# SwiGLU by Strassen products: the weight sums moved from GpSimd to VectorE, with more places for the first weight parts, later splits, and the last tile done for both halves at once

## The chip, the cores and the metric

The kernel runs on one core of one Trainium2 chip. The metric is the device time of one execution in microseconds (us). TensorE (PE) multiplies matrices, VectorE (DVE), ScalarE (ACT) and GpSimd (POOL) work on tiles in SBUF, SyncE (SP) issues most DMAs; GpSimd issues some too. Each engine runs its own instructions in a fixed order and waits on semaphores for the others.

## The reference

One inference step of a two-layer decoder trunk: layer 0 mixes tokens with an mLSTM, layer 1 with latent attention, and each is followed by a dense SwiGLU FFN. The part that matters here is the FFN, on T = 1032 tokens (1024 of a prompt and 8 of decoding requests), D_MODEL = 1024, D_FF = 2816, all in float32:

```python
def rmsnorm(x, g):
    x32 = x.astype(jnp.float32)
    y = x32 * lax.rsqrt(jnp.mean(x32 * x32, axis=-1, keepdims=True) + EPS)
    return (y * g.astype(jnp.float32)).astype(x.dtype)

def swiglu(x, w_gate_up, w_down):
    g, u = jnp.split(x @ w_gate_up, 2, axis=-1)
    return (jax.nn.silu(g) * u) @ w_down
...
        hp = hp + swiglu(rmsnorm(hp, norm_ffn[layer]), ffn_w_gate_up[layer], ffn_w_down[layer])
        hs = hs + swiglu(rmsnorm(hs, norm_ffn[layer]), ffn_w_gate_up[layer], ffn_w_down[layer])
```

## The kernel before

**Precision.** A float32 value is kept as a high part and a low part. `split` makes them: ScalarE copies the value rounded to the high part (L117), VectorE subtracts it to get the low one (L118). Each product is then three matmuls (`mm3`): high × high (L134), high × low of the activations (L135), low of the weights × high (L136). So the third matmul of a group can start only when VectorE's subtract is done, while the first two need only ScalarE's copy.

**Halves and tiles.** The tokens are in two halves of 512 and 520, each of two columns (256 and 260 wide, `PW`). D_FF is cut into 22 tiles of 128 (`NF`), named f = 0 to 21. The layer's normalised activations are made by a generator (`forms`) as seven sums and differences per half, each split: f0 to f6 hold half 0 (f7 also serves), c0 to c5 hold half 1.

**Gate and up, one tile.** `gate_up(wg, f, parts)` computes gate and up of a tile by seven Strassen products (`PRODUCTS`) instead of eight. For each product four pieces of k run through `mm3`, for half 0 and then for half 1, into the PSUM banks `sc`. So a tile for both halves is 7 × 2 × 4 × 3 = 168 matmuls. The results are gathered by ScalarE's copies and VectorE's additions into the tiles `u` and `gt` (L1050 to L1064), and silu and the product are applied there.

**Weights.** `operands` (L986 on) is a generator that yields the seven weight parts of a tile in the order of the products. It issues two loads of 512 KB on SyncE's queue into tiles `wr` (a11, a12 of the gate in the first, a21, a22 of up in the second). Four sums of 128x512 are formed: s = a21 + a22 (L1007), s3 = a11 − a21 (L1008), s − a11 (L1012) and a12 − s (L1015), all on GpSimd, called S in the rows. s and s3 need the second load. Each part is split by `put` into a place of 128 × 1024; there are three places, two of tag `wh` and one of tag `w3`, taken in turn, so a part's split waits for the end of the product that used the place three parts earlier. In the rows, places print as `wh`, `w` (that is `w3`) and `wl`. `gate_up` keeps one part made ahead of the product that runs.

**Down.** `down` is a generator over 36 steps of 14 products of `mm3` each (again Strassen, on pairs of f tiles), with operands `dA` to `dD` (weights loaded as `dr`, sums dS L1093 to L1096) and b (factors made from u by `spread`, L1072 to L1078, and split). Its PSUM banks are `mm` and `ss`, emptied at L1132 to L1143 into `wl` (two tiles of the tag `wl`, called st0) and `st`, and added to the result in DRAM by accumulating DMAs that GpSimd issues (L1144). `gate_up` calls it between its own products: after every second piece of k (a checkpoint) it takes one or more entries.

**The order of the FFN** (`ffn`): tiles 0 and 1 for half 0 are done before it, while the norm of half 1 is made. Then tile 2 for both halves, tiles 0 and 1 for half 1, tile 3 for both halves with the first two steps' entries of `down` (skip the first checkpoint, then two a checkpoint), tiles 4 to 19 with one entry a checkpoint, the rest of `down`. The last four tiles (18 to 21) are not fed to `down`: `keep` splits their u whole into tiles `a`, and plain down products (`last_products`) follow, in `to_mla` for layer 0 and `finish` for layer 1. Layer 1's tile 21 is done for half 0 and then again for half 1, with the loads, sums and splits of its weights each time; layer 0's is done once for both halves.

The instructions' order on each engine is set by a scheduler from the order of the code, its own costs and the tiles' places.

Of the kernel before, what the change touches and what calls it, by code (L numbers as in the profile page):

```python
# [28 lines left out]
NF = DFF // P  # L29
# [62 lines left out]
class Kern:  # L92
# [896 lines left out]
    def operands(self, wg, f):  # L989
        nc = self.nc  # L990
# [7 lines left out]
        def put(x):  # L998
            self.no += 1
            pool, tag = (self.wp, "wh") if self.no % 3 else (self.gu, "w3")  # L1000
            w = self.t(pool, [P, KT * P], tag, F32R).rearrange("p (i k m) -> p i k m", i=2, m=P)
            self.split(w[:, 0], w[:, 1], x)
            return w

        G = nc.gpsimd.tensor_tensor
        s, s3 = (self.t(self.gu, [P, 4, P], "S", bufs=2) for i in range(2))
# [13 lines left out]

    def gate_up(self, wg, f, parts, down=iter(()), skip=0, steps=1):
        nc = self.nc
        V = nc.vector
        gu = self.gu
        banks = {}
        U, X = {}, {}
        ops = self.operands(wg, f)
        ahead = next(ops)
        for s, bank, first in PRODUCTS:
            w, ahead = ahead, next(ops, None)  # L1030
            for i in parts:
# [5 lines left out]
                for k in range(4):  # L1037
                    self.mm3(ps, w[:, 0, k], w[:, 1, k], xh[:, k], xl[:, k], bool(first) and k == 0, k == 3, skip_group_check=True)
                    if k % 2:
                        if skip:  # L1040
                            skip -= 1
                        else:
                            for _ in range(steps):
                                next(down, None)
                if s == 0:
# [111 lines left out]
    def ffn(self, layer):  # L1157
# [12 lines left out]
        g = self.down(wd)  # L1170
        next(g)
        self.gate_up(wg, 3, (0, 1), g, 1, 2)
        for f in range(4, NF - 2):
# [8 lines left out]
        def keep(f, i):  # L1182
            o = lambda x: x[:, 512 * i:512 * i + 2 * PW[i]].rearrange("p (c t) -> p c t", c=2)
            self.split(o(self.act[f][0]), o(self.act[f][1]), self.u[f, i])

        for f in fs[:2]:
            for i in range(2):
                keep(f, i)
        for f in fs[2:]:
            for parts in ((0,), (1,)) if layer and f == NF - 1 else ((0, 1),):  # L1190
                self.gate_up(wg, f, parts)
                for i in parts:
                    keep(f, i)
        self.fc.release()
# [822 lines left out]
```

## Time and profile before

| | us |
|---|---|
| median of 3 runs | 2763.43 |
| lowest, highest | 2760.77, 2763.75 |
| profiled execution | 2736.87 |
| its span (first to last instruction) | 2735.1 |
| mean granted TensorE clock | 0.972 |
| FFN of layer 0 from tile 2 on (start of its products) | from 548.6 |
| FFN of layer 1 likewise | from 2015 |
| layer 1's tile 21 | 2639.25 to 2669.76 |

The profile is of one execution, and 1.8 us of it lie outside the span. A timeline row gives the start, the duration, the engine, the line, the operation, its output and inputs, the count, and in brackets the idle time before it and what ended that. Matmuls overlap, so a matmul's cost is the distance between starts and not its duration. A row of windows gives per engine the busy time and the count of instructions.

### The profile page before, as it was taken

How to read it: one execution, taken by the hardware profiler on the slowest of the kernel's cores; microseconds unless marked ns; L12 is line 12 of the kernel's file. 1: busy time of each engine (PE TensorE's matmuls, PEld its weight loads, DVE VectorE, ACT ScalarE, POOL GpSimd, SP SyncE). 2: the span in 40 equal slices, each digit the busy share in tenths (PEclk: the TensorE clock that was granted, in tenths of full speed). 3: DMA queues.
4: the chain of work that ended last, by engine and by line, in shares of the span. 5: the costliest groups of instructions: out<-in, count | busy, mean ns of one | idle time of the engine just before them, and what ended most of it. 6: DMA issues, size and time to landing. Idle time of an engine off the chain costs nothing. (4 is left out here: it accounts for less than half of the span.)

```text
span 2735.1 us, 54524 instructions
## 1 busy us (share of the span) xinstructions
PE 2553.6 (93%) x21151; PEld 2398.4 (88%) x21151; DVE 1884.8 (69%) x4321; ACT 1320.8 (48%) x3287; POOL 824.9 (30%) x762
## 2 busy tenths in 40 slices
PE   8999998979999999999889889888989999999988
PEld 8998976979999999999877677677988999999988
DVE  4345668868777778666558777685676877777755
ACT  4212334446555555454345464555345555555542
POOL 1000102223333333322336454442223333333332
PEclk9999989999999999999989999899999999999999
DMA  5133454416565655643667776555424566655652
GB/s 186 39 77 89 127 147 115 154 51 128 117 129 113 132 110 112 125 154 98 229 222 270 260 261 209 202 206 168 137 71 104 113 124 127 121 117 117 128 132 102
DMA packets 344073, 384.43 MB, mean 141 GB/s; under 512 B 23449, under 2 KB 276766, under 8 KB 335494
## 3 DMA queue, kind: packets, MB, share of 16 engines
q0 software_dynamic: 59520, 183.34, 28.6%
q1 hardware_dynamic: 259894, 181.25, 22.1%
q10 hardware_dynamic: 24400, 16.36, 2.3%
q8 instruction: 166, 2.72, 0.4%
q14 instruction: 93, 0.76, 0.1%
HBM read 255.17 MB, written 125.70 MB: 139 GB/s over the span
## 5 line engine op out<-in xcount | busy, mean ns | idle before, releaser
L117 ACT ACTIVATE wh<-wr 128x512 fp32r<-128x512 f32 (+2 forms) x176 | 141.4, 804 | 224.4 <-PE mm L135 129.5
L1144 POOL DMA_DIRECT2D x_d<-wl x72 | 86.7, 1204 | 315.3 <-DVE wl L1143 250.0
L1795 DVE STREAM_TRANSPOSE tt<-nat 128x1024 f32<-128x1024 f32 x128 | 153.6, 1222 | 13.1 <-DMA nat<-in_cache_latent_dram,idx 6.9
L118 DVE TENSOR_TENSOR b<-u,b 128x256 fp32r<-128x256 f32 (+1 forms) x252 | 135.5, 542 | 16.7 <-ACT b L117 16.7
L1007 POOL TENSOR_TENSOR S<-wr 128x512 f32<-128x512 f32 x45 | 70.1, 1559 | 254.7 <-DMA wr<-in_ffn_w_gate_up_dram 230.5
L1012 POOL TENSOR_TENSOR S<-S,wr 128x512 f32<-128x512 f32 x45 | 63.0, 1401 | 245.0 <-DVE wh L118 166.2
L118 DVE TENSOR_TENSOR wl<-wr,wh 128x1024 fp32r<-128x1024 f32 (+2 forms) x83 | 99.2, 1195 | 42.7 <-ACT wh L117 30.9
L117 ACT ACTIVATE b<-u 128x256 fp32r<-128x256 f32 (+1 forms) x252 | 98.4, 415 | 43.0 <-DVE u L1060 15.4
L118 DVE TENSOR_TENSOR wh<-S,wh 128x512 fp32r<-128x512 f32 x121 | 86.2, 712 | 34.7 <-ACT wh L117 32.8
L134 PE MATMUL mm<-zh,wh 128*128 128x344 f32 x320 | 104.3, 326 | 4.2 <-DVE ot L462 4.2
L135 PE MATMUL mm<-zl,wh 128*128 128x344 f32 x320 | 103.6, 324 | 0.0
L136 PE MATMUL mm<-zh,wl 128*128 128x344 f32 x320 | 103.3, 323 | 0.0
L1144 POOL DMA_DIRECT2D x_d<-st x72 | 99.9, 1388 | 7.0 <-ACT b L117 6.1
L117 ACT ACTIVATE wh<-S 128x512 fp32r<-128x512 f32 x121 | 76.5, 633 | 48.1 <-PE sc L136 28.6
L1802 PE MATMUL ss<-tt,qbd 128*32 128x128 f32 x2560 | 88.2, 279 | 8.6 <-DVE tt L1795 7.0
L1802 PEld LDWEIGHTS ss<-tt,qbd 128*32 128x32 f32 x2560 | 70.9, 111 | 21.5 <-DVE tt L1795 15.9
L1093 DVE TENSOR_TENSOR dS<-dr 128x128 f32<-128x128 f32 x72 | 48.0, 667 | 59.4 <-DMA dr<-in_ffn_w_down_dram 56.6
L1698 PE MATMUL mm<-wh,vt 128*128 128x256 f32 (+1 forms) x320 | 76.9, 302 | 10.7 <-ACT wh L117 6.0
L134 PE MATMUL sc<-zh,wh 128*128 128x344 f32 x256 | 84.0, 329 | 0.2 <-DVE q L432 0.2
L850 POOL TENSOR_TENSOR ss<-ss,sq 128x512 f32<-128x512 f32 (+2 forms) x36 | 49.5, 1374 | 113.4 <-ACT sq L849 113.1
L135 PE MATMUL sc<-zl,wh 128*128 128x344 f32 x256 | 83.0, 324 | 0.0
L136 PE MATMUL sc<-zh,wl 128*128 128x344 f32 x256 | 82.9, 324 | 0.0
(1002 smaller groups left out, 10949.6 us busy)
## 6 DMA issues: line engine op xcount, KB each, us to landing
wr<-in_ffn_w_gate_up_dram SPq DMA_DIRECT2D x98, 512.0 KB
x_d<-st POOLq DMA_DIRECT2D x72, 520.0 KB, 8.4
x_d<-wl POOLq DMA_DIRECT2D x72, 512.0 KB, 6.2
dr<-in_ffn_w_down_dram SPq DMA_DIRECT2D x72, 256.0 KB
wr<-in_mlstm_w_in_dram SPq DMA_DIRECT2D x24, 512.0 KB
wr<-in_mlstm_w_out_dram SPq DMA_DIRECT2D x16, 512.0 KB
wr<-in_mla_w_o_dram SPq DMA_DIRECT2D x15, 512.0 KB
q<-qn_d SPq DMA_DIRECT2D x28, 256.0 KB
```

Source lines behind the costliest of these rows:

```text
L117: ins = nc.scalar.activation(hi, src, AF.Copy)
L118: self.low = e.tensor_tensor(lo, src, hi.bitcast(F32), op=ALU.subtract)
L134: mm(ps, wh, xh, start=start, stop=False, **kw)
L135: mm(ps, wh, xl, start=False, stop=False, **kw)
L136: self.last = mm(ps, wl, xh, start=False, stop=stop, **kw)
L850: (V if d == KT - 1 else nc.gpsimd).tensor_tensor(SS[:, cs], SS[:, cs], sq, op=ALU.add)
L1007: G(s, a21, a22, op=ALU.add)
L1012: G(s, s, a11, op=ALU.subtract)
L1144: nc.gpsimd.dma_start(self.x_d[:, 2 * dp:2 * dp + 2, 512 * i:512 * i + 2 * PW[i]], st[i], accum_op=ALU.add)
L1698: nc.tensor.matmul(o, x, y, start=i == 0, stop=i == len(ops) - 1)
L1795: V.transpose(out=tt, in_=src.rearrange("p s (c i) -> p c s i", i=32))
L1802: nc.tensor.matmul(psS[32 * j:32 * j + 32, u * P:u * P + P], self.qbd[:, b, cb], tt[:, c, 4 * j:4 * j + 4].rearrange("p s k -> p (s k)"), ...
```

## The change

1. The four sums of `operands` are made by VectorE (`G = nc.vector.tensor_tensor`). GpSimd keeps its DMAs.
2. For tiles 0, 1 and 2 (f < 3) the parts go to five places in turn instead of three: `wh`, `wl`, `w3`, `wh`, `wl`; the two `wl` tiles are those that `down` takes for its results later. For these tiles two parts are made ahead, for the others one. The other tiles have the same three places as before.
3. In tile 3, `down` starts after five checkpoints, at 54 entries to 23 checkpoints, instead of after one at two a checkpoint.
4. The splits of the four last tiles: tile 18 is split ahead of tile 20, tile 19 within tile 20, tiles 20 and 21 after tile 21; before, 18 and 19 ahead of tile 20, and 20 and 21 each behind its own products.
5. Layer 1's tile 21 is done for both halves at once. Its weights are loaded, summed and split once.

The lines of the functions shift by two or three: L1007, L1008, L1012, L1015 are L1009, L1010, L1014, L1017; L1050 is L1053, L1058 to L1064 are L1061 to L1067, L1139 is L1142.

```diff
@@ -997,12 +997,14 @@
         def put(x):
             self.no += 1
-            pool, tag = (self.wp, "wh") if self.no % 3 else (self.gu, "w3")
+            tags = ("wh", "wl", "w3", "wh", "wl") if f < 3 else ("wh", "w3", "wh")
+            tag = tags[self.no % len(tags)]
+            pool = self.gu if tag == "w3" else self.wp
             w = self.t(pool, [P, KT * P], tag, F32R).rearrange("p (i k m) -> p i k m", i=2, m=P)
             self.split(w[:, 0], w[:, 1], x)
             return w
 
-        G = nc.gpsimd.tensor_tensor
+        G = nc.vector.tensor_tensor
         s, s3 = (self.t(self.gu, [P, 4, P], "S", bufs=2) for i in range(2))
         G(s, a21, a22, op=ALU.add)
         G(s3, a11, a21, op=ALU.subtract)
@@ -1018,16 +1020,18 @@
-    def gate_up(self, wg, f, parts, down=iter(()), skip=0, steps=1):
+    def gate_up(self, wg, f, parts, down=iter(()), skip=0, steps=(1, 1)):
...
+        cp = done = 0
         ops = self.operands(wg, f)
-        ahead = next(ops)
+        ahead = [next(ops) for _ in range(2 if f < 3 else 1)]
         for s, bank, first in PRODUCTS:
-            w, ahead = ahead, next(ops, None)
+            ahead.append(next(ops, None))
+            w = ahead.pop(0)
...
                     if k % 2:
-                        if skip:
-                            skip -= 1
-                        else:
-                            for _ in range(steps):
-                                next(down, None)
+                        cp += 1
+                        while done * steps[1] < steps[0] * (cp - skip):
+                            next(down, None)
+                            done += 1
@@ -1169,7 +1172,7 @@
-        self.gate_up(wg, 3, (0, 1), g, 1, 2)
+        self.gate_up(wg, 3, (0, 1), g, 5, (54, 23))
@@ -1183,14 +1186,13 @@
-        for f in fs[:2]:
+        for i in range(2):
+            keep(fs[0], i)
+        self.gate_up(wg, fs[2], (0, 1), (keep(fs[1], i) for i in range(2)))
+        self.gate_up(wg, fs[3], (0, 1))
+        for f in fs[2:]:
             for i in range(2):
                 keep(f, i)
-        for f in fs[2:]:
-            for parts in ((0,), (1,)) if layer and f == NF - 1 else ((0, 1),):
-                self.gate_up(wg, f, parts)
-                for i in parts:
-                    keep(f, i)
```

How the order of the instructions moves, at three places. First VectorE at the start of layer 0's tile 2, before: c5l is the last low part of the norm that the place begins with, `wh` the low part of a11 and later of a12, b and u belong to the factors of `down`. A row is line, operation, output, inputs, size, and the engines waited for.

```order
L118 TENSOR_TENSOR c5l_5586<-x_4738,c5h_5585 128x1040 [waits Activation_49]
L118 TENSOR_TENSOR wh_5636<-wr_5628,wh_5636 128x512 [waits DMAHW2_49]
L118 TENSOR_TENSOR b_5603<-u_5286,b_5603 128x256 [waits Activation_49]
L118 TENSOR_TENSOR b_5607<-u_5438,b_5607 128x256 [waits Activation_49]
L1072 TENSOR_TENSOR u_5286<-u_5286 128x256 [waits DVE_49]
L118 TENSOR_TENSOR b_5625<-u_5438,b_5625 128x256 [waits Activation_49]
L1076 TENSOR_TENSOR u_5286<-u_5438,u_5286 128x256 [waits DVE_49]
L118 TENSOR_TENSOR b_5610<-u_5286,b_5610 128x256 [waits Activation_49]
L118 TENSOR_TENSOR wh_5639<-wr_5628,wh_5639 128x512
```

The same place in the changed kernel, where a11's low part is written to a place of the tag `wl`:

```order
L1009 TENSOR_TENSOR S_5632<-wr_5630 128x512 [waits DMAHW3_49]
L118 TENSOR_TENSOR b_5603<-u_5286,b_5603 128x256 [waits Activation_49]
L118 TENSOR_TENSOR b_5607<-u_5438,b_5607 128x256 [waits Activation_49]
L1075 TENSOR_TENSOR u_5286<-u_5286 128x256 [waits DVE_49]
L118 TENSOR_TENSOR b_5625<-u_5438,b_5625 128x256 [waits Activation_49]
L1079 TENSOR_TENSOR u_5286<-u_5438,u_5286 128x256 [waits DVE_49]
L118 TENSOR_TENSOR b_5610<-u_5286,b_5610 128x256 [waits Activation_49]
L1010 TENSOR_TENSOR S_5633<-wr_5628,wr_5630 128x512 [waits DMAHW2_49]
L1077 TENSOR_TENSOR u_5286<-u_5438,u_5286 128x256 [waits DVE_49]
L118 TENSOR_TENSOR b_5619<-u_5286,b_5619 128x256 [waits Activation_49]
L1081 TENSOR_TENSOR u_5438<-u_5438,u_5286 128x256 [waits DVE_49]
L118 TENSOR_TENSOR wl_5636<-wr_5628,wl_5636 128x512
```

a11's low part, directly behind c5l before, now stands behind the two sums and nine operations on b and u.

Second, VectorE in a steady tile of layer 0, before (this is the place at 829.6 us of the trace; `wh_9228` is the low part of the next tile's a11, `w_9231` that of a12, L1139 empties a bank of `down`):

```order
L1058 TENSOR_TENSOR u_8882<-u_8882,sc_8915 128x260 [waits Activation_49]
L118 TENSOR_TENSOR wh_9228<-wr_9220,wh_9228 128x512 [waits DMAHW6_49,Activation_49]
L118 TENSOR_TENSOR dA_9138<-dr_9056,dA_9138 128x256 [waits Activation_49]
L1060 TENSOR_TENSOR u_8846<-u_8846,sc_8817 128x256 [waits PE_49]
L118 TENSOR_TENSOR b_9141<-u_8846,b_9141 128x256 [waits Activation_49]
L118 TENSOR_TENSOR b_9153<-u_8440,b_9153 128x256 [waits Activation_49]
L1060 TENSOR_TENSOR u_8882<-u_8882,sc_8849 128x260 [waits PE_49]
L118 TENSOR_TENSOR w_9231<-wr_9220,w_9231 128x512 [waits Activation_49]
L118 TENSOR_TENSOR b_9168<-u_8482,b_9168 128x260 [waits Activation_49]
L118 TENSOR_TENSOR dB_9182<-dS_9058,dB_9182 128x256 [waits Activation_49]
L1139 TENSOR_TENSOR wl_6158<-wl_6158,ss_9048 128x256 [waits Activation_49]
```

And in the changed kernel, where `wr_9222` is the second load:

```order
L1009 TENSOR_TENSOR S_9224<-wr_9222 128x512 [waits DMAHW0_49]
L118 TENSOR_TENSOR dA_9138<-dr_9056,dA_9138 128x256 [waits Activation_49]
L1010 TENSOR_TENSOR S_9225<-wr_9220,wr_9222 128x512 [waits DMAHW6_49]
L1063 TENSOR_TENSOR u_8846<-u_8846,sc_8817 128x256 [waits PE_49]
L118 TENSOR_TENSOR wh_9228<-wr_9220,wh_9228 128x512
L118 TENSOR_TENSOR b_9141<-u_8846,b_9141 128x256 [waits Activation_49]
L118 TENSOR_TENSOR b_9153<-u_8440,b_9153 128x256 [waits Activation_49]
L1063 TENSOR_TENSOR u_8882<-u_8882,sc_8849 128x260 [waits PE_49]
L118 TENSOR_TENSOR wh_9231<-wr_9220,wh_9231 128x512 [waits Activation_49]
L118 TENSOR_TENSOR b_9168<-u_8482,b_9168 128x260 [waits Activation_49]
L118 TENSOR_TENSOR dB_9182<-dS_9058,dB_9182 128x256 [waits Activation_49]
L1142 TENSOR_TENSOR wl_6158<-wl_6158,ss_9048 128x256 [waits Activation_49]
```

S, which waits for the second load, stands where a11's low part was, and ahead of everything down to the emptied bank.

Third, ScalarE in layer 0's tile 20, before: S_13375 and S_13376 are sums of the tile's weights, the four `a` are the splits of tiles 18 and 19, and the copies to u free the banks of the tile's first product.

```order
L117 ACTIVATE w_13421<-S_13375 128x512 [waits PE_49,Pool_49]
L117 ACTIVATE wh_13481<-S_13376 128x512 [waits PE_49,Activation_49]
L117 ACTIVATE a_13355<-u_12600 128x512
L117 ACTIVATE a_13355<-u_12642 128x520
L117 ACTIVATE a_13357<-u_13006 128x512
L117 ACTIVATE a_13357<-u_13042 128x520 [waits DVE_49]
L1050 COPY u_13398<-sc_13385 128x256 [waits DVE_49]
```

And in the changed kernel:

```order
L117 ACTIVATE wh_13421<-S_13371 128x512 [waits DVE_49,PE_49,Activation_49]
L117 ACTIVATE w_13481<-S_13372 128x512 [waits PE_49,Activation_49]
L117 ACTIVATE a_13355<-u_12600 128x512
L117 ACTIVATE a_13355<-u_12642 128x520
L117 ACTIVATE a_13357<-u_13006 128x512
L117 ACTIVATE a_13357<-u_13042 128x520
L1053 COPY u_13398<-sc_13381 128x256 [waits DVE_49]
```

The four splits stand where they stood, ahead of the copy.

## The prediction

> **What bounds the kernel now.** I read the head of the page first: TensorE (PE) is busy almost all of the span, VectorE (DVE) two thirds, GpSimd (POOL) a third.
>
> ```profile
> span 2735.1 us, 54524 instructions
> PE 2553.6 (93%) x21151; PEld 2398.4 (88%) x21151; DVE 1884.8 (69%) x4321; ACT 1320.8 (48%) x3287; POOL 824.9 (30%) x762
> ```
>
> So an edit can only win the places where PE stands still or runs at half clock. To price a matmul at full speed I took a stretch of TensorE's timeline without waits, the last weight tile (21) of layer 0, 168 matmuls:
>
> ```profile
> 1174.03 0.28 PE L134 MATMUL sc<-f0h,wh 128*128 128x256 f32 x1
> 1194.05 0.32 PE L134 MATMUL sc<-a,wh 128*128 128x344 f32 x1
> ```
>
> 20.02 us / 168 = 0.119 us each. With that I priced two stretches by windows (columns: window, its length, then busy us and count of PE, weight loads, DVE, ACT, POOL): the start of layer 0's FFN, and sixteen of its later tiles.
>
> ```profile
> 548.60:617.00 68.40, 52.07 (x381) 49.76 (x379) 46.90 (x82) 29.92 (x66) 17.57 (x14) 0.90 0.18 51
> 640.00:1140.00 500.00, 491.20 (x4060) 484.77 (x4060) 384.12 (x903) 283.78 (x777) 170.16 (x132) 1.00 0.62 122
> ```
>
> The start needs 381 × 0.119 = 45.3 us and takes 68.4: 23 us are lost. The steady part needs 4060 × 0.119 = 483 of 500: 17 us lost, about 1 us a tile. So the start of each layer is the worst place, and a steady tile has next to nothing to give.
>
> **The start (two parts ahead, five places; sums on VectorE).** TensorE's timeline names the waits (the bracket is the idle time before a row and its releaser):
>
> ```profile
> 548.61 0.28 PE L134 MATMUL sc<-f0h,wh 128*128 128x256 f32 x1
> 548.97 0.28 PE L135 MATMUL sc<-c0l,wh 128*128 128x260 f32 x1
> 553.16 0.58 PE L134 MATMUL sc<-f4h,wh 128*128 128x256 f32 x1 [3.91 <-ACT wh L117]
> 557.07 0.58 PE L136 MATMUL sc<-f0h,wh 128*128 128x256 f32 x1 [2.69 <-DVE wh L118]
> 561.49 0.28 PE L134 MATMUL mm<-b,dA 128*128 128x256 f32 x1
> 565.64 0.38 PE L134 MATMUL sc<-f3h,wh 128*128 128x256 f32 x1 [0.77 <-ACT wh L117]
> 576.07 0.39 PE L136 MATMUL sc<-f5h,w 128*128 128x256 f32 x1 [1.73 <-DVE w L118]
> 585.76 0.39 PE L134 MATMUL sc<-c3h,wh 128*128 128x260 f32 x1 [1.04 <-ACT wh L117]
> 600.74 0.39 PE L134 MATMUL sc<-c3h,w 128*128 128x260 f32 x1 [3.38 <-ACT w L117]
> 617.02 0.39 PE L134 MATMUL mm<-b,dB 128*128 128x260 f32 x1 [2.83 <-ACT b L117]
> ```
>
> These waits make 16.4 us; from 557.07 to 561.49 the 20 matmuls after the first take 4.42 us instead of 2.5, half clock. The rest of the 23 is a second half-clock stretch behind the 3.38 and small bubbles. What comes of them? The first low part (a11's subtract) is on VectorE, here:
>
> ```profile
> 555.19 1.23 DVE L118 TENSOR_TENSOR c5l<-x,c5h 128x1040 fp32r<-128x1040 f32 x1
> 556.34 0.68 DVE L118 TENSOR_TENSOR wh<-wr,wh 128x512 fp32r<-128x512 f32 x1
> 556.94 0.41 DVE L118 TENSOR_TENSOR b<-u,b 128x256 fp32r<-128x256 f32 x1
> 557.61 0.41 DVE L1072 TENSOR_TENSOR u<-u 128x256 f32<-128x256 f32 x1
> 557.95 0.41 DVE L118 TENSOR_TENSOR b<-u,b 128x256 fp32r<-128x256 f32 x1
> ```
>
> In the changed order this subtract stands eleven rows later, behind S, S3 and nine 256-wide operations. At 0.60 us from start to start for the 512-wide (556.34 to the next row's 556.94) and 0.34 for the others, it starts at 556.34 + 2 × 0.60 + 9 × 0.34 = 560.6 and ends at 561.2, where it ended at 557.0. TensorE has eight matmuls of high parts to run from 548.6 (1.0 us) and then stands until 561.2: 11.6 us idle where it was 6.6, with 1.9 us of half clock behind it. So the edit makes the first wait worse by 5. What it buys comes after: with two parts made ahead and no part waiting for the place of one in use, the waits at 565.64, 576.07 and 585.76 go, and the down steps, which now begin after 5 checkpoints instead of 1, no longer ask for spread factors at 617.02 before ScalarE has them. Of the 3.38 I keep half (1.7), an estimate: that part's load lands no earlier. Loss after: 11.6 + 1.9 + 1.7 = 15.2 of 23, a gain of 7.8; I take 7.5. Ends: if only the added wait comes true, −5; if the kept 1.7 goes as well, +9.5. Layer 1 starts with the same two waits,
>
> ```profile
> 2019.72 0.58 PE L134 MATMUL sc<-f4h,wh 128*128 128x256 f32 x1 [3.94 <-ACT wh L117]
> 2023.63 0.58 PE L136 MATMUL sc<-f0h,wh 128*128 128x256 f32 x1 [2.69 <-DVE wh L118]
> ```
>
> so 2 × 7.5 = **15 us**.
>
> **The sums in a steady tile.** The groups of the page and of GpSimd's lines (after the bar: busy us, mean ns, then idle time before):
>
> ```profile
> L1008 POOL TENSOR_TENSOR S<-wr,wr 128x512 f32<-128x512 f32 x45 | 72.5, 1610 | 0.0
> L1007 POOL TENSOR_TENSOR S<-wr 128x512 f32<-128x512 f32 x45 | 70.1, 1559 | 254.7 <-DMA wr<-in_ffn_w_gate_up_dram 230.5 <-DVE gt L1062 17.4 <-DVE u L1060 6.8
> L118 DVE TENSOR_TENSOR wh<-S,wh 128x512 fp32r<-128x512 f32 x121 | 86.2, 712 | 34.7 <-ACT wh L117 32.8
> ```
>
> A sum of 128x512 costs GpSimd 1.6 us; VectorE does the same shape in 0.71, or 0.60 from start to start. Four new ones a tile are 2.4 to 2.8 us. But they also take something off it. In one tile of layer 0, VectorE's rows, then GpSimd's:
>
> ```profile
> 829.64 0.42 DVE L1058 TENSOR_TENSOR u<-u,sc 128x260 f32<-128x260 f32 x1
> 833.97 1.67 DVE L118 TENSOR_TENSOR w<-wr,w 128x512 fp32r<-128x512 f32 x1 [0.23 <-ACT w L117]
> 835.56 1.53 DVE L118 TENSOR_TENSOR b<-u,b 128x260 fp32r<-128x260 f32 x1
> 837.35 0.41 DVE L1139 TENSOR_TENSOR wl<-wl,ss 128x256 f32<-128x256 f32 x1
> 841.66 1.52 DVE L1064 TENSOR_TENSOR u<-u,gt 128x260 f32<-128x260 f32 x1
> ```
>
> ```profile
> 833.77 1.32 POOL L1007 TENSOR_TENSOR S<-wr 128x512 f32<-128x512 f32 x1 [6.01 <-DMA wr<-in_ffn_w_gate_up_dram]
> 835.04 1.77 POOL L1008 TENSOR_TENSOR S<-wr,wr 128x512 f32<-128x512 f32 x1
> 841.49 1.41 POOL L1012 TENSOR_TENSOR S<-S,wr 128x512 f32<-128x512 f32 x1 [4.68 <-DVE wh L118]
> ```
>
> While a sum runs, VectorE's subtract takes 1.67 instead of 0.7, and 260-wide operations 1.53 and 1.52 instead of 0.42: 1.0 + 1.1 + 1.1 = 3.2 us lost in this tile. The load of VectorE is therefore about even, 2.8 in and 3.2 out.
>
> [...]
>
> The even load is not an even order. S waits for the second weight load: GpSimd stood 6.01 us for it until 833.77, at no cost to anyone. In the changed order VectorE reaches S behind the row of 829.64, so it stands from 830.06 to 833.8, about 3.7 us, and queued behind it are dA's low part, two additions that free PSUM banks, a11's low part, several b's and L1139, which releases the down product's bank. From 833.8 the eleven rows up to L1139, four 512-wide and seven 256-wide, need 4 × 0.60 + 7 × 0.34 = 4.8 us: it comes at 838.6, 1.2 later than 837.35. Behind it the stretch of 1.1 us at 841.66 is gone, which sits just ahead of this wait of TensorE:
>
> ```profile
> 843.57 0.39 PE L134 MATMUL ss<-b,dA 128*128 128x256 f32 x1 [0.77 <-DVE wl L1143]
> ```
>
> So a wash tile by tile: at best this 0.8, at worst the 1.2. I take +1 per layer, **2 us**; the ends, sixteen tiles at the one or the other, are −19 and +12 per layer, and are the first two rivals below.
>
> **The last tiles.** Layer 1's last tile goes half by half, each half with its own loads, sums and splits; in the changed kernel once for both, as layer 0 has it.
>
> ```profile
> 2639.25 0.28 PE L134 MATMUL sc<-f0h,wh 128*128 128x256 f32 x1
> 2659.70 0.39 PE L134 MATMUL sc<-c3h,wh 128*128 128x260 f32 x1 [4.33 <-ACT wh L117]
> 2669.76 0.34 PE L134 MATMUL sc<-a,wh 128*128 128x384 f32 x1
> ```
>
> 30.51 us for the 168 matmuls that layer 0 does in 20.02: 10.5 us. I take off 1 for the S that VectorE now runs ahead of that tile's first low parts: **9.5 us**, ends 7 and 11. The last down products behind it wait for the same loads as before.
>
> Splits put later: in layer 0, TensorE stands before tile 20's third product for ScalarE's copy (L1050):
>
> ```profile
> 1158.12 0.39 PE L134 MATMUL sc<-f3h,w 128*128 128x256 f32 x1 [3.12 <-ACT u L1050]
> ```
>
> The code moves two of the four splits into tile 20, but ScalarE's order leaves all four ahead of that copy, as before. The wait stays: 0, and −0.5 for VectorE's sums there.
>
> **Sum.** 15 + 2 + 9.5 − 0.5 = 26 us. The profiled execution took 2736.87 (the span and 1.8 around it), 26.6 below the median of 2763.43; it would take 2710.9, and the median 2737.4. I carry the difference, not the ratio.
>
> **The rivals.**
>
> *VectorE behind the load (slower).* The 3.7 us stand for S is not made up: the bank-freeing additions L1058 to L1064 and L1139 come so late that TensorE waits in most tiles. For it: VectorE's 384 us of 500 plus 3.7 × 16 = 59 is 89%. Against it: 1.2 us is all that the chain above delays. It decides from 0.75 us a tile on: 32 tiles × 0.75 = 24 us eat the other terms. At 1.2 us a tile it costs 38, so 2763.4 − 24 + 38 = 2777. Chance 0.13. [...]
>
> *VectorE freed (faster still).* The stretches were what cost the steady 17 us per layer; without them 8 to 10 per layer come back beyond my 1: 2737 − 18 = 2719. For it: the 0.77 wait at 843.57 stands behind a stretched row. Chance 0.18.
>
> *The start gives nothing.* The longer first wait uses up what the five places bring; only the last tile is left: 2763.4 − 9.5 = 2754, or 2757 with the steady part a little late. Chance 0.15.
>
> *Nothing happens as said* (the gains are given back in the down products behind the FFN): 2761. Chance 0.05.
>
> My forecast, gains of 18 to 33 us: 0.49.
>
> **The numbers.** The range runs from 2717 (the freed VectorE) to 2757 (the start gives nothing); outside lie the slower case, the last rival and a little below. A difference of 0.2%, 5.5 us, is about what a measurement of this kernel can tell from none. Faster by more: 0.49 + 0.18 + 0.15 and less a little for partial losses, 0.79; within: 0.08; slower: 0.13.
>
> **What would show it.** Right: one idle stretch of 11 to 12 us soon after 548.6, then no wait over 2 us up to the next two tiles; VectorE's 260-wide operations at 0.42 throughout; waits of 3 to 4 us on VectorE before S; layer 1's last tile at 20 to 21.5 us; the 3.1 us wait in tile 20 still there. Wrong: steady windows of the same 4060 matmuls longer or shorter than 500 us by over 10, or a start as long as 68 us.

## The result, and the profile after

The changed kernel takes 2722.52 us (median of 4 runs, 2715.67 to 2727.58) against 2762.44 (4 runs, 2760.77 to 2763.75): a ratio of 0.9857, 95% interval 0.984 to 0.9874, 40 us faster. The forecast was 2737.4, 26 us faster, with a range of 2717 to 2757.

The two profiled executions cannot be set side by side as wholes: their spans, 2735.1 and 2725.8, differ by 9 only, because the profile of before fell 26 us under its runs' median. The difference lies outside the FFN. From layer 0's tile 21 to layer 1's tile 2 (one tile, the last products and layer 1's mixer, none of them changed in what it runs) before's profile has 841.1 us and after's 863.4; the profiles of the twelve later runs have 834 to 848 there, so it is after's that stands out. So I compare stages of the FFN, cut at the first matmul of a tile. First before, by windows (length, then busy us and count of PE, weight loads, DVE, ACT, POOL, then TensorE's granted clock): layer 0's start up to tile 4, its tiles 4 to 19, its tile 20; layer 1's start, its tiles 4 to 19, and its tile 21 up to the end.

```profile
548.61:651.61 103.00, 86.65 (x668) 84.14 (x667) 72.73 (x153) 53.06 (x130) 28.96 (x23) 0.93 0.37 81
651.61:1149.11 497.50, 488.70 (x4041) 482.32 (x4039) 379.04 (x887) 279.74 (x764) 165.80 (x128) 1.00 0.61 120
1149.11:1174.03 24.92, 21.80 (x170) 21.59 (x169) 11.21 (x22) 9.31 (x21) 8.07 (x6) 0.93 0.42 86
2015.13:2119.11 103.98, 88.67 (x668) 86.15 (x667) 73.09 (x152) 53.63 (x131) 29.84 (x23) 0.92 0.37 82
2119.11:2615.82 496.71, 488.90 (x4040) 482.52 (x4039) 378.90 (x888) 279.66 (x762) 163.84 (x128) 1.00 0.61 120
2639.25:2735.10 95.85, 80.37 (x548) 76.41 (x546) 52.53 (x98) 32.80 (x65) 28.99 (x28) 0.95 0.38 127
```

The same stages after:

```profile
555.04:648.90 93.86, 84.13 (x669) 82.69 (x668) 73.98 (x172) 53.64 (x129) 7.35 (x6) 0.95 0.40 89
648.90:1143.04 494.14, 485.06 (x4040) 482.17 (x4039) 363.85 (x950) 284.33 (x764) 77.89 (x64) 1.00 0.61 121
1143.04:1169.00 25.96, 22.83 (x171) 22.62 (x169) 13.50 (x26) 9.22 (x21) 2.44 (x2) 0.87 0.41 82
2032.41:2124.10 91.69, 82.86 (x668) 81.42 (x667) 73.45 (x170) 53.45 (x129) 7.38 (x6) 0.96 0.41 92
2124.10:2616.78 492.68, 484.72 (x4041) 481.20 (x4039) 364.14 (x951) 283.69 (x764) 77.87 (x64) 1.00 0.62 121
2641.63:2725.80 84.17, 76.27 (x548) 74.54 (x546) 44.95 (x93) 28.49 (x58) 19.48 (x21) 0.97 0.41 133
```

The counts of matmuls agree, so the lengths compare like with like: the starts are 9.1 and 12.3 us shorter, tiles 4 to 19 3.4 and 4.0, the end 11.7; tile 20 is 1.0 longer in layer 0 and 1.4 in layer 1 (23.43 to 24.85). Together 38 us, which is the measured 40 but for 2. VectorE does 63 operations more in tiles 4 to 19 and is busy 15 us less, 364 instead of 379: it gained the sums and lost the stretches.

The start in the changed kernel, on TensorE, to hold against the ten rows of the prediction:

```profile
563.75 0.58 PE L134 MATMUL mm<-b,dA 128*128 128x256 f32 x1 [7.13 <-ACT dA L117]
565.54 0.58 PE L136 MATMUL sc<-f0h,wl 128*128 128x256 f32 x1 [0.57 <-DVE wl L118]
606.02 0.38 PE L134 MATMUL sc<-f0h,w 128*128 128x256 f32 x1 [1.11 <-ACT w L117]
```

One stand of 7.7 us broken by four down matmuls, then no wait over 0.2 us for 40 us, and then one of 1.11, at tile 3's first product. Layer 1's last tile is one pass, begun at 2641.63; the plain down products behind it begin here:

```profile
2661.64 0.33 PE L134 MATMUL sc<-a,wh 128*128 128x384 f32 x1
```

20.0 us without a wait, where it was 30.5. And VectorE's stand for the load at the tile of the prediction, with what came of it on ScalarE and TensorE:

```profile
828.45 0.69 DVE L1009 TENSOR_TENSOR S<-wr 128x512 f32<-128x512 f32 x1 [3.81 <-DMA wr<-in_ffn_w_gate_up_dram]
830.00 0.41 DVE L1063 TENSOR_TENSOR u<-u,sc 128x256 f32<-128x256 f32 x1
830.45 0.72 ACT L117 ACTIVATE b<-u 128x256 fp32r<-128x256 f32 x2 [4.21 <-DVE u L1063]
832.52 0.35 ACT L1141 COPY wl<-mm 128x256 f32<-128x256 f32 x1
832.92 0.39 PE L134 MATMUL mm<-b,dD 128*128 128x256 f32 x1 [2.13 <-ACT wl L1141]
```

VectorE stands 3.81 us; L1063, queued behind S, is late; ScalarE stands 4.21 for it with its copy L1141 queued behind; TensorE stands 2.13 for that copy.

### The profile page after: what moved, and what is told of

Same layout as the page of the kernel before. It is cut to its first block, busy times and chain, and to the rows that moved or that the text cites. A ratio compares the mean times of both kernels' runs of the same rounds, so it can differ in the third digit from the quotient of the medians.

```text
span 2725.8 us, 54325 instructions
## 1 busy us (share of the span) xinstructions
PE 2538.9 (93%) x21151; PEld 2389.8 (88%) x21151; DVE 1859.1 (68%) x4490; ACT 1327.4 (49%) x3280; POOL 576.3 (21%) x582
## 3 DMA queue, kind: packets, MB, share of 16 engines
q1 hardware_dynamic: 257814, 180.21, 22.2%
## 4 chain that ended last, share of the span: by engine, by line
PE 62%; DVE 16%; DMA 11%; ACT 5%; issue 3%; POOL 1%; another core or an unknown queue 0%; SPq 0%; ACTq 0%; POOLq 0%; DVEq 0%
PE sc L136 12%; PE sc L134 11%; PE sc L135 11%; PE mm L134 5%; PE mm L136 5%; PE mm L135 4%; DMA wr<-in_ffn_w_gate_up_dram 3%; DVE tt L1797 2%; PE ss L1829 2%; DMA Gb<-G_d 2%; PE ss L134 2%; PE ss L136 2%; PE ss L135 2%; DVE wl L118 2%; PE ss L1804 1%
## 5 line engine op out<-in xcount | busy, mean ns | idle before, releaser
L1804 PE MATMUL ss<-tt,qbd 128*32 128x128 f32 x2560 | 92.7, 281 | 17.2 <-DVE tt L1797 12.2
L118 DVE TENSOR_TENSOR b<-u,b 128x256 fp32r<-128x256 f32 (+1 forms) x252 | 104.6, 422 | 1.4 <-ACT b L117 1.3
L117 ACT ACTIVATE wh<-S 128x512 fp32r<-128x512 f32 x108 | 68.3, 633 | 47.7 <-PE sc L136 33.4
L118 DVE TENSOR_TENSOR wh<-S,wh 128x512 fp32r<-128x512 f32 x108 | 74.2, 689 | 22.1 <-ACT wh L117 21.0
L134 PE MATMUL sc<-zh,wh 128*128 128x344 f32 x256 | 84.1, 329 | 1.3 <-ACT wh L117 1.1
L118 DVE TENSOR_TENSOR wh<-wr,wh 128x512 fp32r<-128x512 f32 x85 | 58.5, 688 | 26.5 <-ACT wh L117 26.4
L1659 ACT ACTIVATE wr<-sc,mx,rqt 128x512 f32<-128x512 f32 (+2 forms) x96 | 64.1, 673 | 22.5 <-DVE mx L1654 12.6
L1700 PEld LDWEIGHTS mm<-wh,vt 128*128 128x128 f32 x320 | 56.1, 197 | 21.6 <-ACT wh L117 8.7
L1789 POOL DMA_INDIRECT nat<-in_cache_latent_dram,idx x64 | 61.2, 957 | 61.8 <-PE ss L1829 48.2
```

The source lines that it names most:

```text
L117: ins = nc.scalar.activation(hi, src, AF.Copy)
L118: self.low = e.tensor_tensor(lo, src, hi.bitcast(F32), op=ALU.subtract)
L134: mm(ps, wh, xh, start=start, stop=False, **kw)
L1659: nc.scalar.activation(px[:, ks], o, AF.Exp, bias=mx[:, 0:1], scale=f, accum_out=sm[:, c:c + 1])
L1700: nc.tensor.matmul(o, x, y, start=i == 0, stop=i == len(ops) - 1)
L1789: nc.gpsimd.indirect_dma_start(out=nat[:, s].rearrange("p s c -> p (s c)"), out_offset=None, in_=lat, in_offset=ix)
```

## The experiments

The theory from the stages: the starts gain by quick sums and by places together, the steady tiles a little by VectorE not being held up, the end by one pass instead of two. The first rival: the sums on VectorE are the whole of the start, and the places do little. The table has every run's stages, cut as above. "Idle" is the sum of TensorE's waits over 0.2 us in both starts, from the timeline; it moves less from run to run than the starts' lengths, since the half-clock stretches (told of at the end) vary: the same code of the start has 103.0 and 104.0 us in the kernel before and 103.7 and 99.0 with only the last tile changed, with 31.7 and 29.5 idle.

| kernel | starts | idle | tiles 4 to 19 | tile 20 | 21 to end | time, before there |
|---|---|---|---|---|---|---|
| before | 103.0, 104.0 | 31.7 | 497.5, 496.7 | 24.9, 23.4 | 95.9 | |
| changed | 93.9, 91.7 | 18.5 | 494.1, 492.7 | 26.0, 24.9 | 84.2 | 2722.5, 2762.4 |
| changed, again | 92.3, 92.2 | 17.1 | 493.0, 492.4 | 24.9, 23.4 | 84.2 | 2693.1, 2735.7 |
| sums back | 95.8, 97.4 | 22.2 | 495.5, 496.1 | 24.7, 26.0 | 83.9 | 2709.1, 2732.5 |
| places back | 96.5, 98.2 | 22.7 | 493.1, 492.2 | 23.4, 23.4 | 84.3 | 2705.7, 2732.5 |
| end back | 93.8, 93.0 | 17.8 | 493.1, 492.3 | 24.9, 24.9 | 94.1 | 2700.6, 2732.5 |
| sums only | 98.4, 95.5 | 20.2 | 495.8, 495.7 | 24.9, 25.0 | 93.2 | 2717.9, 2732.5 |
| late sums | 90.0, 89.4 | 12.3 | 489.2, 488.4 | 24.9, 25.9 | 84.6 | 2683.3, 2735.7 |
| early down | 96.8, 95.9 | 21.8 | 493.5, 491.5 | 24.7, 24.9 | 84.1 | 2700.3, 2735.7 |
| last tile only | 103.7, 99.0 | 29.5 | 495.7, 495.8 | 23.4, 23.4 | 85.5 | 2721.9, 2735.7 |
| two sums on GpSimd | 93.7, 93.3 | 18.3 | 496.1, 497.0 | 24.9, 23.4 | 85.3 | 2698.8, 2733.5 |
| the same, late start | 90.1, 90.3 | 12.2 | 496.1, 496.7 | 24.9, 26.2 | 83.8 | 2692.8, 2733.5 |
| one part ahead | 92.3, 91.1 | 17.1 | 493.3, 493.1 | 24.9, 24.9 | 84.8 | 2693.3, 2733.5 |
| steady sums on GpSimd | 93.2, 92.7 | 17.3 | 497.0, 497.0 | 24.9, 23.4 | 84.2 | 2698.8, 2733.5 |

The first two rows are the pair of the result. The other runs were made later, in three sets on chips 4 and 11 (the pair's chip is not known); there the kernel before takes 2732 to 2736 us and not 2762, about what its profiled execution took. So each time stands beside the kernel before of its own set.

### The sums back on GpSimd

```diff
-        G = nc.vector.tensor_tensor
+        G = nc.gpsimd.tensor_tensor
```

> The changed kernel with the four sums back on GpSimd; places, later down, splits and last tile stay as changed. The changed kernel's trace against before's: start (from tile 2's first product to tile 4's) 93.9 instead of 103.0 us in layer 0, 91.7 instead of 104.0 in layer 1; tiles 4 to 20 520.1 instead of 522.4 and 517.5 instead of 520.1; from tile 21 of layer 1 to the end 84.2 instead of 95.9. My theory: the start's 21 us come from the places, the second part made ahead and the later down; the sums bring the steady 5 and at most 6 of the start. So starts of 92 to 97 us, steady as before, time 2728 to 2734. Rival (the sums themselves make the start, since GpSimd is slow and holds VectorE up): starts back at 103 to 104, time about 2748.

Ratio 0.991 (0.9892 to 0.9928), 23 us under the kernel before, where my theory had 28 to 34: the sums are worth more than I gave them. Still the starts come back by 2 to 6 us, not by ten, so the rival falls; the steady tiles give back 1.4 and 3.4. There is one thing in it that I had not seen. VectorE's last low part of the norm (c5l) starts 6.6 to 6.9 us after tile 2's first matmul in the kernel before and in this one, which leave the first sums to GpSimd, and 4.2 to 4.4 us after it wherever they are on VectorE. ScalarE's rows show why, in this kernel:

```profile
545.19 0.64 ACT L117 ACTIVATE wh<-S 128x512 fp32r<-128x512 f32 x1 [2.77 <-POOL S L1009]
545.73 1.06 ACT L117 ACTIVATE c2h<-x 128x1040 fp32r<-128x1040 f32 x1
```

A split of S stands in ScalarE's queue ahead of the norm's split c2h, and GpSimd's sum (3.2 us there) is late. VectorE then waits for c2h: in the kernel before it stood 2.5 us for it.

```profile
549.09 1.24 DVE L118 TENSOR_TENSOR c2l<-x,c2h 128x1040 fp32r<-128x1040 f32 x1 [2.50 <-ACT c2h L117]
```

### The places back

```diff
-            tags = ("wh", "wl", "w3", "wh", "wl") if f < 3 else ("wh", "w3", "wh")
+            tags = ("wh", "w3", "wh")
-        ahead = [next(ops) for _ in range(2 if f < 3 else 1)]
+        ahead = [next(ops) for _ in range(1)]
```

> The changed kernel with three places for every tile and one part made ahead; sums on VectorE, later down, splits and last tile stay. My theory: starts back at 100 to 104 us in both layers, time about 2740 to 2745. Rival (the sums make the start): starts stay at 92 to 96, time 2722 to 2728.

Ratio 0.9905 (0.9873 to 0.9937). Starts 96.5 and 98.2: between the two, and idle 22.7 against 17 to 18.5. So neither theory had it alone. With the later down in all three, sums without places leave 22.7, places without sums 22.2, both 17 to 18.5; with none of the three 29.5 to 31.7. Either, with the later down, takes 7 to 9.5 us of idle time out of the two starts, both together 11 to 15: they take the same waits away in part. What the later down does in this is told with the run that begins it early.

### The end back

```diff
-        for i in range(2):
-            keep(fs[0], i)
-        self.gate_up(wg, fs[2], (0, 1), (keep(fs[1], i) for i in range(2)))
-        self.gate_up(wg, fs[3], (0, 1))
-        for f in fs[2:]:
-            for i in range(2):
-                keep(f, i)
+        for f in fs[:2]:
+            for i in range(2):
+                keep(f, i)
+        for f in fs[2:]:
+            for parts in ((0,), (1,)) if layer and f == NF - 1 else ((0, 1),):
+                self.gate_up(wg, f, parts)
+                for i in parts:
+                    keep(f, i)
```

> The changed kernel with the splits of the last tiles and layer 1's last tile in two halves as before; the rest stays. My theory: from layer 1's tile 21 to the end 94 to 96 us instead of 84.2, all else equal, time 2733 to 2735. Rival (the tail's gain came half from VectorE's quicker sums, which ended the wait of 4.33 us): about 90 us, time 2727 to 2729.

Ratio 0.9878 (0.9862 to 0.9895). The end takes 94.1 us, as foreseen: with quick sums the two passes need 28.4 us instead of 30.5, and the last products behind them 65.7 instead of 64.2. Nothing else moves: tile 20 keeps its wait of 3.1 us with the splits as before or as changed, in every kernel of the table.

### The sums only

```diff
-        G = nc.gpsimd.tensor_tensor
+        G = nc.vector.tensor_tensor
```

(in the kernel before)

> The kernel before with only the four sums moved to VectorE. My theory: steady 5 us less over both layers, start 0 to 6 less, last tile at most 2 less: time 2750 to 2758. Rival (the sums make the start): starts at 92 to 96, time about 2736.

Ratio 0.9938 (0.9916 to 0.996), 14.6 us under; the profile has 17 over its stages: 13 in the starts, 1 to 1.7 in each steady part, 2.7 at the end, less 1.5 in tile 20. The starts gained more than I gave the sums; layer 1's 95.5 lies in the rival's range, layer 0's 98.4 does not. That the steady part gained is not shown by this run: with only the last tile changed, where the steady tiles run the same rows as before, they take 495.7 and 495.8 too.

### The changed kernel again

> The changed kernel unaltered, to stand beside the kernels of this call and to show how far stages move from run to run. Theory: start to tile 4 91 to 95 us in both layers, tiles 4 to 19 492 to 495, tile 20 23.4 to 26 (the 3.1 us wait, with or without half clock behind it), tail 84; time some 38 to 40 us under the kernel before of the same chip. Rival (the first run's gap of 40 us was in part chance of that chip): under 33 us.

Ratio 0.9844 (0.9824 to 0.9864), 42.6 us under, and the stages repeat to within 1.6 us. The first result was no chance of one set of runs.

### Later sums

```diff
-        G(s, a21, a22, op=ALU.add)
-        G(s3, a11, a21, op=ALU.subtract)
         yield put(a11)
         yield put(a12)
+        G(s, a21, a22, op=ALU.add)
         s1 = put(s)
         G(s, s, a11, op=ALU.subtract)
         yield put(s)
         yield s1
+        G(s3, a11, a21, op=ALU.subtract)
         G(s, a12, s, op=ALU.subtract)
```

> The changed kernel with S made after a11 and a12 are split, and S3 just before it is split: on VectorE a11's low part follows c5l at once at the start, and in steady tiles a11's and dA's low parts stand ahead of S, the rest still behind it. My theory (the first wait is a11's low part standing behind the sums): first waits 4 instead of 7.7 us, start 3 to 4.5 us shorter in each layer, steady 0 to 2 shorter per layer: 6 to 12 us under the changed kernel. Rival (the later parts are what bounds the start, so that time won at the first wait is waited later): start as in the changed kernel, time within 3 us of it.

2683.3 us (2676.1 to 2686.0), ratio 0.9808 (0.9782 to 0.9834): 9.8 us under the changed kernel of the same set, whose runs (2690.3 to 2700.5) do not overlap it. This version beats both kernels. At the start a11's low part follows c5l at once and the one wait is 4.70 us:

```profile
551.85 0.58 PE L136 MATMUL sc<-f0h,wl 128*128 128x256 f32 x1 [4.70 <-DVE wl L118]
```

Idle falls by 5 to 6 us over the two starts, a little less than I expected, and none of it is waited later, so the rival falls. In tiles 4 to 19 it wins 4 us a layer, twice the most that I expected. The view of waits for layer 0's tiles 4 to 19 (us in total, times, longest), changed kernel first:

```profile
PE mm L134 <- ACT wl L1141: 5.0, 4, 2.1
PE sc L134 <- ACT wh L117: 2.2, 4, 0.7
```

and with later sums:

```profile
PE sc L134 <- ACT wh L117: 2.4, 5, 0.6
PE mm L134 <- ACT wl L1141: 0.9, 1, 0.9
```

It is the wait for L1141, the end of the chain shown above, that goes. In most steady tiles a11's and dA's low parts moved ahead of S, and the addition L1063 that the chain waited for moved ahead of the second sum. VectorE still stands for the load, 11 times and 18.6 us in these tiles, where the changed kernel has 12 and 30.1.

### Down begun as early as before

```diff
-        self.gate_up(wg, 3, (0, 1), g, 5, (54, 23))
+        self.gate_up(wg, 3, (0, 1), g, 1, (2, 1))
```

> The changed kernel with down begun after one checkpoint of tile 3 at two a checkpoint, as before. My theory: the wait for b's at tile 3 comes back only in part, since VectorE's sums are quick: 1 to 3 us more in each start, 2 to 6 in all. Rival (the later down does nothing once the places are there): within 1.5 us of the changed kernel.

2700.3 us, 7.2 above the changed kernel of its set; the starts are 3.7 to 4.5 longer each, more than the 1 to 3 that I expected. Idle in the starts is 21.8 against 17.1: one wait of 2.2 to 2.4 us in each layer's tile 3, for the addition L1142 that empties a down bank. The reason that I gave is wrong: the b's are in time. It is VectorE behind the load again, here the load of tile 4's weights, with L1142 queued behind the sum:

```profile
628.07 0.69 DVE L1009 TENSOR_TENSOR S<-wr 128x512 f32<-128x512 f32 x1 [4.40 <-DMA wr<-in_ffn_w_gate_up_dram]
630.56 0.41 DVE L1142 TENSOR_TENSOR wl<-wl,ss 128x256 f32<-128x256 f32 x1
631.02 0.38 PE L134 MATMUL ss<-b,dC 128*128 128x256 f32 x1 [2.38 <-DVE wl L1142]
```

The sums only, with `down` as early and three places, have the same wait (1.8 to 1.9 us behind a stand of 3.5 to 3.8). Read beside each other, the runs with quick sums show that the places and the later `down` are worth something only together: the two starts take 193.9 us with neither (sums only), 192.6 with the places alone (this run), 194.6 with the later `down` alone (places back), and 183.4 to 186.8 with both, in the four profiles that have both with quick sums throughout. The first three differ by no more than repeats do.

### The last tile only

```diff
-            for parts in ((0,), (1,)) if layer and f == NF - 1 else ((0, 1),):
+            for parts in ((0, 1),):
```

(in the kernel before)

> The kernel before with only layer 1's last tile done for both halves at once (sums on GpSimd). My theory: from tile 21 to the end 84 to 86 us instead of 95.9, so 10 to 12 us under the kernel before. Rival (the sums on GpSimd hold the one pass up as they held the half: a wait of 4 us stays): 88 to 90, 6 to 8 us under.

The end takes 85.5 us, 10.3 less; the medians differ by 13.8, ratio 0.9971 (0.9941 to 1.0002), an interval that takes in no difference; the stage is what shows the gain. With GpSimd's sums the single pass runs in 20.0 us too, so the rival falls: one pass does not wait for them.

### Two sums on GpSimd

```diff
-        G(s, a21, a22, op=ALU.add)
-        G(s3, a11, a21, op=ALU.subtract)
+        H = nc.gpsimd.tensor_tensor if f > 3 else G
+        H(s, a21, a22, op=ALU.add)
+        H(s3, a11, a21, op=ALU.subtract)
```

> The changed kernel with S and S3 of tiles 4 to 21, the two sums that wait for the second load, on GpSimd; the other two on VectorE. So VectorE never stands for a load, but is stretched while S and S3 run. My theory (the stand makes ScalarE's copy L1141 late, on which TensorE's first down matmul waits): those waits fall from 3 to 5 us per layer to under 1, small waits return by half; tiles 4 to 19 489 to 492 us per layer against 493, time 2 to 8 under the changed kernel. Rival (what GpSimd holds up by its sums costs as much as the stand): 493 to 496 per layer, 0 to 6 above the changed kernel.

2698.8 us, ratio 0.9896 (0.9849 to 0.9943); tiles 4 to 19 take 496.1 and 497.0. The length came out at the rival's upper end or just above (493 to 496 per layer). VectorE no longer stands for the load and the waits for that copy (L1142 there) are down to 1.6 us from 5.0, as my theory had it, but others took their place; layer 0's tiles 4 to 19:

```profile
PE sc L134 <- ACT wh L117: 4.1, 5, 1.1
PE sc L134 <- ACT w L117: 1.6, 3, 0.6
```

One of them, TensorE behind ScalarE behind VectorE:

```profile
773.17 0.38 PE L134 MATMUL sc<-f3h,wh 128*128 128x256 f32 x1 [0.82 <-ACT wh L117]
772.48 0.63 ACT L117 ACTIVATE wh<-S 128x512 fp32r<-128x512 f32 x1 [1.16 <-DVE S L1015]
```

The sum waited for is the third, s − a11 (L1015 there), which stayed on VectorE and comes late in its queue. So this kernel shows that the load's wait can be taken off VectorE, and not what GpSimd's sums alone cost.

### The same with late sums at the start

```diff
+        H = nc.gpsimd.tensor_tensor
+        if f > 3:
+            H(s, a21, a22, op=ALU.add)
+            H(s3, a11, a21, op=ALU.subtract)
...
+        if f <= 3:
+            G(s, a21, a22, op=ALU.add)
         s1 = put(s)
...
+        if f <= 3:
+            G(s3, a11, a21, op=ALU.subtract)
```

> As the kernel with late sums for tiles 0 to 3 (S behind a11 and a12, S3 before its split, on VectorE), and S and S3 of tiles 4 to 21 on GpSimd. My theory: starts 89 to 91, as with late sums; tiles 4 to 19 489 to 492, no better than the 489 of late sums, where a11's and dA's low parts stand ahead of S already: time 0 to 6 above the kernel with late sums. Rival (the rest of the stand still costs): tiles 4 to 19 under 487.

2692.8 us, ratio 0.9861 (0.9828 to 0.9893). Starts 90.1 and 90.3 and idle 12.2, as with late sums on VectorE; tiles 4 to 19 at 496.1 and 496.7, as with two sums on GpSimd: worse than I expected, and the two effects add up independently. It is 40.7 us under the kernel before, where the later sums alone are 52.3 under.

### One part ahead

```diff
-        ahead = [next(ops) for _ in range(2 if f < 3 else 1)]
+        ahead = [next(ops) for _ in range(1)]
```

> The changed kernel with the five places but only one part made ahead in tiles 0 to 2. My theory: the places do the work, the second part ahead is worth up to 2 us a start: 92 to 95 us, time 0 to 4 above the changed kernel. Rival (the second part ahead is what the places are for): starts 96 to 98 as without both, 7 to 12 above.

2693.3 us, ratio 0.9847 (0.9818 to 0.9877); starts 92.3 and 91.1, idle 17.1. The second part made ahead is worth nothing; of the two, it is the five places that count.

### The steady sums on GpSimd

```diff
-        G = nc.vector.tensor_tensor
+        G = (nc.vector if f < 3 else nc.gpsimd).tensor_tensor
```

> The changed kernel with all four sums of tiles 3 to 21 on GpSimd, those of tiles 0 to 2 on VectorE. My theory: starts stay at 92 to 95; tiles 4 to 19 back at 495 to 497 per layer (TensorE's many waits under 0.2 us come back, those for L1141 go): 4 to 8 above the changed kernel. Rival (the start's gain needs the sums of tile 3 and the steady part too): starts at 95 to 98, 10 to 16 above.

2698.8 us, ratio 0.9881 (0.985 to 0.9911). The starts stay (93.2, 92.7); tiles 4 to 19 take 497.0 in both layers, 2.8 to 4.7 more than in the two runs of the changed kernel. The waits of 0.2 us are back, in layer 0:

```profile
PE ss L134 <- DVE st L1146: 1.6, 7, 0.2
PE ss L134 <- DVE st L1137: 1.4, 7, 0.2
```

The kernel before has the same fourteen; the changed one has none.

```profile
PE ss L134 <- DVE st L1143: 1.6, 7, 0.2
PE ss L134 <- DVE st L1134: 1.5, 7, 0.2
```

So the start needs the sums of tiles 0 to 2 on VectorE, and the steady gain needs those of the others.

## Why the prediction came out as it did

The direction was right and the time lay in the range. Three gains and the one loss came out larger than foreseen: 21.4, 7.4 and 11.7 us for 15, 2 and 9.5, and 2.5 lost in the tiles 20 for 0.5. Of the mechanisms, the longer way to a11's low part, VectorE's stand for the load, the single pass and the unmoved wait in tile 20 came as worked out. What the start's other waits were put down to did not, nor did the path by which the stand costs time; that the time lay inside the range, 5.5 us above its lower bound, is in part luck.

**The start: 15 foreseen, 21.4 in the profiles.** That a11's low part would stand eleven rows later was right to the tenth: from S to that part VectorE takes 564.80 − 560.58 = 4.2 us.

```profile
559.43 1.23 DVE L118 TENSOR_TENSOR c5l<-x,c5h 128x1040 fp32r<-128x1040 f32 x1
560.58 0.68 DVE L1009 TENSOR_TENSOR S<-wr 128x512 f32<-128x512 f32 x1
564.80 0.69 DVE L118 TENSOR_TENSOR wl<-wr,wl 128x512 fp32r<-128x512 f32 x1
```

The step that failed is the one that set this piece behind an unmoved c5l: "it starts at 556.34 + ...". c5l comes 4.39 us after tile 2's first matmul and no longer 6.58, since the sum that ScalarE stood for is gone. I had costed the sums by what they add to VectorE's queue, and not by what waited for GpSimd's. From tile 2's first matmul to the first that uses a low part it is 10.5 us, where I had 12.6; c5l's 2.2 are that difference. After it there is one wait of 1.1 us, where I had kept 1.7 for another. Of the 21.4, 13.2 is idle time. The other 8.2 fits half clock, which I had put at 1.9 after the first wait and left out of the difference elsewhere: the granted clock is 0.5 for 30.7 us of the two starts before and for 17.1 after, and half the difference is 6.8, an estimate.

The reason that I gave, two parts ahead and the places, was half of it. Quick sums alone, with three places and `down` as early as before, leave 20.2 us idle of 31.7, and the second part ahead takes nothing away. The steps that failed are the reasons given for the waits at 600.74 ("that part's load lands no earlier") and at 617.02 (the early `down`). Both stand behind GpSimd's sums, through ScalarE's splits:

```profile
600.06 0.63 ACT L117 ACTIVATE w<-S 128x512 fp32r<-128x512 f32 x1 [2.07 <-POOL S L1012]
612.98 0.63 ACT L117 ACTIVATE w<-S 128x512 fp32r<-128x512 f32 x1 [2.48 <-POOL S L1007]
```

With the sums only neither wait is there, though `down` begins as early and VectorE still stands 0.95 us for that part's load.

**The steady tiles: 2 foreseen, 7.4 up to tile 19.** VectorE's stand came as worked out, 3.7 foreseen and 3.81 here, the longest; in layer 0's tiles 4 to 20 it is 13 stands, 30.3 us.

```profile
DVE S L1009 <- DMA wr<-in_ffn_w_gate_up_dram: 30.3, 13, 3.8
```

The price of the wait at L1139 was wrong in kind. I looked for it on VectorE's addition behind a dozen rows, and it came through ScalarE, which stood for L1063 with the copy L1141 behind it. Yet the sum is a gain, because the fourteen waits of 0.2 us per layer that GpSimd's stretches made are gone. Each stands behind an addition that VectorE reaches late, after an operation that ran 1.52 or 1.53 us beside the third sum, or 1.42 to 1.44 beside the fourth, where 0.42 is usual (before's layer 0). The idle time does not show it: over these tiles TensorE has 8.8 and 7.8 us before, 9.1 and 8.0 after. From start to start it does:

```profile
719.46 0.28 PE L136 MATMUL sc<-f4h,wh 128*128 128x256 f32 x1
719.97 0.39 PE L134 MATMUL ss<-b,dA 128*128 128x260 f32 x1 [0.23 <-DVE st L1143]
720.20 0.28 PE L135 MATMUL ss<-b,dA 128*128 128x260 f32 x1
```

The distances are 0.51 and 0.23 us where 0.12 is usual. Over the fourteen the excess is about 6.8 us a layer, where the view has 3.1 us of waits. With the steady sums on GpSimd the two layers take 497.0 each, with them on VectorE 492.4 to 494.1. So two of the rivals were true at once, with opposite signs: VectorE freed, worth 8 us a layer (497.0 with GpSimd's sums to the later sums' 489), and VectorE behind the load, which takes 4 of them back (489 to 493). The second is 0.25 us a tile, a third of the 0.75 from which it would have decided. The trace shows the stretches that the first rests on gone, and not what made them: VectorE's low parts of b average 422 ns where they averaged 542, before first.

```profile
L118 DVE TENSOR_TENSOR b<-u,b 128x256 fp32r<-128x256 f32 (+1 forms) x252 | 135.5, 542 | 16.7 <-ACT b L117 16.7
L118 DVE TENSOR_TENSOR b<-u,b 128x256 fp32r<-128x256 f32 (+1 forms) x252 | 104.6, 422 | 1.4 <-ACT b L117 1.3
```

What stays open: with the sums only, tiles 4 to 19 take 495.8 and 495.7, with the sums and the other edits 492 to 494. The three kernels that undo one other edit (places, end, early down) have the changed kernel's order in these tiles, row for row on TensorE, VectorE and ScalarE, and its times, 491.5 to 493.5. With the sums only, TensorE's order differs in the first tile alone, but VectorE's in 132 of its 948 rows in layer 0; S stands up to 12 rows earlier or later. So the 2 to 4 us go with the order that the scheduler made; which rows cost them is not shown.

**The end: 9.5 foreseen, 11.7 in the profiles.** The 10.5 of the second pass came in full, 30.51 to 20.0; the 1 that I took off for S did not come, and the last products behind it are 1.2 shorter. The one-edit run gives 10.3 for the stage, its reversal, with the splits, 9.9.

**The later splits: 0 foreseen, and −0.5 for tile 20.** The wait of 3.13 us in tile 20 stays, since the order on ScalarE did not change. At the end they are worth something that I left out: layer 1's last products take 65.3 to 65.7 us in the four kernels with the earlier splits and 63.8 to 65.2 in the ten with the later ones. The 2.5 us that the two tiles 20 lost in this profile have a reason told below; in the second run of the changed kernel they lost nothing.

## What to carry to other kernels

When work is taken off a slow engine (GpSimd: 1.3 to 1.6 us for a sum that takes VectorE 0.69), look for those that wait for it in other queues: what I missed at the start was a split of the norm, queued on ScalarE behind a split that waited for GpSimd's sum, and two more waits of the same kind. When it is put on a busy engine, where one row's wait holds up the rows queued behind it (3.81 us of VectorE here), place what waits for a transfer behind what does not: a few rows moved ahead of the sums were worth 10 us here. And undo a change's parts both ways, each alone and each taken out, because parts that remove the same wait look worth more alone than together, and parts that need each other look worth nothing alone.

## What the runs showed of the hardware that I had not expected

The same wait of 3.13 us is sometimes followed by half clock and sometimes not. In the changed kernel's tile 20:

```profile
1152.02 0.58 PE L134 MATMUL sc<-f3h,wh 128*128 128x256 f32 x1 [3.13 <-ACT u L1053]
1152.40 0.41 PE L135 MATMUL sc<-f3l,wh 128*128 128x256 f32 x1
1152.62 0.41 PE L136 MATMUL sc<-f3h,wh 128*128 128x256 f32 x1
```

With the places back, the same row of the same order:

```profile
1145.74 0.39 PE L134 MATMUL sc<-f3h,wh 128*128 128x256 f32 x1 [3.13 <-ACT u L1053]
1145.96 0.29 PE L135 MATMUL sc<-f3l,wh 128*128 128x256 f32 x1
1146.08 0.29 PE L136 MATMUL sc<-f3h,wh 128*128 128x256 f32 x1
```

0.22 us from start to start against 0.12. It makes tile 20 23.4 us in one case and up to 26.2 in the other, and it is why tile 20 looks longer in the changed kernel.

The traces show where the two cases differ. In each profile all stretches at half clock begin on one grid of 3.413 us; those in the changed kernel's FFNs begin at 560.54, 833.61, 1151.05, 2038.51 and 2625.61, which are 80, 93, 260 and 172 steps apart. In the FFNs of the pair they last 3.41, 6.83 or 10.24 us, one to three steps. The grid lies elsewhere in each profile, so the same wait is cut by it differently. Here is the step of the grid in which the wait begins and the stretch that follows, first in the changed kernel, then with the places back. The figure behind the length is TensorE's busy time, and the third from the right is the granted clock:

```profile
1147.63:1151.05 3.42, 1.26 (x11) 1.05 (x9) 1.98 (x4) 2.06 (x4) 0.00 (x0) 1.00 1.10 182
1151.05:1157.88 6.83, 5.86 (x27) 5.86 (x28) 2.38 (x5) 2.61 (x9) 0.00 (x0) 0.50 0.53 125
1140.97:1144.39 3.42, 1.64 (x14) 1.43 (x13) 1.95 (x4) 1.68 (x4) 0.00 (x0) 1.00 1.10 190
1144.39:1147.80 3.41, 2.06 (x17) 2.06 (x18) 2.76 (x6) 2.52 (x7) 0.00 (x0) 1.00 1.04 236
```

The fourteen profiles have 28 of these waits. In 20 of them at least 1.86 us of the wait fall into one step of the grid, and half clock follows each time; in 8 no step holds more than 1.80, and it never follows. The pair has four of them: 2.80 us in before's layer 0 and 2.16 and 2.97 in the changed kernel, each with half clock, and 1.78 in before's layer 1, without. Shorter waits do it too: the 2.13 us shown above leave TensorE busy for 1.29 us of the step from 830.19 to 833.61, and 3.41 us of half clock follow. So in these waits 1.86 us of idle time, a little over half a step, was enough each time. What sets the grid is not shown.

And the kernel before takes 2762 us in the runs of the first pair and 2732 to 2736 in the three later sets, on chips 4 and 11. The changed kernel's two profiled executions differ by 27 us, and their FFN stages by at most 1.6 each: a difference between executions of different sets says little about a change unless it is taken stage by stage.
